# The first stage of a decoder block on one core: products nobody reads ahead of the tokens, earlier weight requests, a projection in three sweeps, forget sums first, values early

## The chip, the cores and the metric

The kernel runs on one core of a Trainium2 chip. The metric is the device time of one execution in microseconds (us). Engines: PE (TensorE), DVE (VectorE), ACT (ScalarE), POOL (GpSimd) and SP (SyncE, which here issues most DMA transfers).

## What is computed

The reference is one decoder block over 512 tokens of 1024 channels, in fp32, with one layer. The first half mixes tokens in three branches and adds the result to x; the second half is an expert retrieval.

```python
h = rmsnorm(x, norm1_g[l])
z = h @ w_in[l]
fq, fk, fv, ff, sq, sk, sv, mq, gl = jnp.split(z, splits, axis=-1)
fq = head_rmsnorm(fq.reshape(B, S, FOX_HEADS, FOX_HD), fox_q_g[l])
fk = head_rmsnorm(fk.reshape(B, S, FOX_HEADS, FOX_HD), fox_k_g[l])
log_f = jax.nn.log_sigmoid((ff + b_forget[l]).astype(jnp.float32))
o_fox = fox_attention(fq, fk, fv, log_f)      # causal, scores + cumsum(log_f)
o_swa = swa_attention(sq, sk, sv, swa_sinks[l], slopes)   # window 128, ALiBi
mn = rmsnorm(mem, mem_norm_g[l])
mk, mv = jnp.split(mn @ w_mem_kv[l], 2, axis=-1)
o_mem = memory_attention(mq, mk, mv)          # 256 memory rows
merged = gates[:, :, 0] * (o_fox @ w_fox_o[l]) + ...
x = x + merged @ w_out[l]
x = x + peer_ffn(rmsnorm(x, norm2_g[l]), ...) # top 16 of 128 x 128 experts, 8 heads
```

## The kernel before

The 512 tokens are four blocks of 128. The mixers run twice: for block 0 alone (group 0) and for blocks 1 to 3 (group 1). The expert search and the fetching of expert rows for block 0 are woven into group 1's mixers; then follow the search for blocks 1 to 3 and a long dense part over all experts for blocks 2 and 3. Up to the end of that search a scheduler with a model of the times sets the order of the instructions on each engine, from the dependences and the order in which the program states them; from the dense part on, PE, DVE and POOL follow the program's own order.

Products that need more than the PE's fast format are made from two parts each: `whi` is the weight rounded by a cast on ACT (`load`, L118), `wlo` the rest, by a subtraction on DVE or POOL (`rest`, L130), and `mm3` (L144 to L146) adds whi x own, wlo x own and whi x ownlo. The weights come as pairs of halves of 512 KB (`raw`, L112); `whi` and `wlo` have three buffers each.

The start of group 0, which the change touches: x of block 0 is fetched, its squares are summed on ACT (`squares`, L197), POOL makes the factor (L191), ACT a diagonal matrix of it (`dg`, L211), and PE turns x by eight products with `dg` (`turn`, L224). ACT and DVE evict each turned chunk into `own` (L225) and `ownlo` (L227). `skvf` then projects to the window keys and values and the eight forget logits (264 columns, w_skvf); its logits become a log-sigmoid (L401 to L404) and a running sum `cum` (L409, L410). `fox_qkv(0, 0)` makes keys, queries and values of the first four forgetting heads (w_nat; 256 columns each); keys and queries carry `cum` as two more columns (L447, L449) and are turned into `kT` and `qT` (L348, L349). `memory` turns the 256 memory rows in the same way as x (`dg` of two blocks, `mT`) and projects them. `fox` attends; `fox_qkv(0, 1)` does the other four heads.

Of the kernel before, what the change touches and what calls it, by code (L numbers as in the profile page):

```python
# [49 lines left out]
AHEAD, ROWS_IN, MORE = 4, 5, 2  # L50
LATER = 400
# [5 lines left out]
def tile_block(ctx: ExitStack, tc: tile.TileContext, t: dict, out: bass.AP):  # L57
# [41 lines left out]
    early, loads = [], [0]  # L99
# [14 lines left out]
    def load(src, n, w, fetch=None):  # L114
# [3 lines left out]
        A.copy(hi[:, :n * w], raw[:, :n * w])  # L118
        return raw[:, :n * w], hi[:, :n * w], n, src.shape[0] if len(src.shape) == 3 else 1
# [15 lines left out]
    def load_split(src, n, w, pool=None, fetch=None):  # L135
        return rest(load(src, n, w, fetch), share[0] if pool is None else pool)
# [37 lines left out]
    nc.sync.dma_start(cst[:, 0], t["c_mats"][:, 0])  # L174
# [62 lines left out]
    first_w = [load_raw(t["w_skvf"][half], 4 * 264) for half in range(2)]  # L237
    nc.sync.dma_start(cst[:, 1:], t["c_mats"][:, 1:])
    pre = ExitStack()
    pp = pre.enter_context(tc.tile_pool(name="pp", bufs=2))  # L240
# [23 lines left out]
    distb = pp.tile([128, 256], BF16, name="distb", bufs=1)  # L264
    slope = pp.tile([128, 8, 128], BF16, name="slope", bufs=1)
    raw = wp.tile([128, WSLOT], F32, tag="raw", name="raw")
    nc.sync.dma_start(raw[:, :256], t["c_dist"])
    V.tensor_copy(distb, raw[:, :256])
    for h in range(8):
        A.mul(slope[:, h], ident, 2.0 ** -(h + 1))  # L270

    def gemm_nat(lhs, src, n, nb, use, more=None, fetch=None):

        w = [load_split(src[half], 4, n, fetch=fetch) for half in range(2)]
# [37 lines left out]
    def heads(lhs, src, nb, nh, hd, pad=0, n=None, also=None, fetch=None):  # L312
# [12 lines left out]

        gemm_nat(lhs, src, n or nh * hd, nb, use, fetch=fetch)
# [58 lines left out]

    def skvf(g, hT):
# [9 lines left out]
        skn = heads(hT, t["w_skvf"], nb, 2, 64, n=264, also=also, fetch=(lambda src, n: first_w.pop(0)) if g == 0 else None)  # L396
# [4 lines left out]
        A.activation(ab, xf[:, bs], AF.Abs)  # L401
        A.activation(ab, ab, AF.Exp, scale=-1.0)
        A.activation(ab, ab, AF.Ln, bias=1.0)
        V.scalar_tensor_tensor(xf[:, bs], xf[:, bs], 0.0, ab, op0=OP.min, op1=OP.subtract)  # L404
        ps = bank("tg")
        for i, b in enumerate(bl):
            for j in range(b):
                PE.matmul(ps[:, i * 8:i * 8 + 8], ones, xf[:, j], start=j == 0, stop=False)
            PE.matmul(ps[:, i * 8:i * 8 + 8], tri, xf[:, b], start=b == 0, stop=True)  # L409
        V.tensor_copy(cum[:, bs].rearrange("p b h -> p (b h)"), ps[:, :nb * 8])  # L410
# [27 lines left out]
    def fox_qkv(g, c, hT):  # L438
# [3 lines left out]
        if g == 0:  # L442
            fkT[c] = pp.tile([128, 4, S], F32, tag="kT", name="kT")
            fv[c] = pp.tile([128, NB, 256], F32, tag="v", name="v")
        kn = heads(hT, t["w_nat"][3 * c], nb, 4, 64, pad=2)
        V.memset(kn[:, :, :, 64], 1.0)
        V.tensor_scalar(kn[:, :, :, 65], cum[:, bs, hs], -1.0, None, op0=OP.mult)  # L447
# [146 lines left out]
    def mixers(g, hT):  # L594
# [731 lines left out]
```

## Time and profile before

| | us |
|---|---|
| median of 3 runs | 1600.31 (1598.24 to 1602.07) |
| the profiled execution, its time | 1592.0 |
| its span in the trace | 1590.2 |
| PE busy | 1506.6 |
| DVE busy | 1427.9 |
| ACT busy | 833.7 |
| PE busy in the first 50 us | 34.1 |

The profile was taken in one execution; "busy" is the time in which an engine ran an instruction, and a row of the timeline gives start, length, engine, source line, operation, output and inputs, and in brackets the engine's idle time before it and what ended that. PE's single rows overlap, since products are pipelined: the pitch from start to start tells its pace. A four-byte product of 128 columns by the slow format appears as two records.

### The profile page before, as it was taken

To read this page: it belongs to the slowest core of one execution; us is meant where nothing else is said; L and a number is where in the kernel's file an instruction comes from. 1 tells how busy PE (TensorE), PEld (TensorE's weight loads), DVE (VectorE), ACT (ScalarE), POOL (GpSimd) and SP (SyncE) were. 2 spreads that over 40 slices of the span, in tenths; PEclk is the share of its full clock that TensorE was granted. 3 is DMA by queue.
4 is the path that set the end of the run, shared out by engine and by line. 5 is a ranking of instruction groups with operands and counts; after the bars stand their busy time and mean duration, and the time that the engine had idled before them with its cause. 6 is when DMAs were issued, how large, how long until landed. Compare 5 with 4: busy or idle time off the path is not lost.

```text
span 1590.2 us, 27117 instructions
## 1 busy us (share of the span) xinstructions
PE 1506.6 (95%) x9422; PEld 1370.9 (86%) x9422; DVE 1427.9 (90%) x2663; ACT 833.7 (52%) x1838; POOL 779.5 (49%) x639
## 2 busy tenths in 40 slices
PE   6999999999998989999995999899999999999998
PEld 5999899898897989999884999688888888888887
DVE  5677477989999989999899999799999999999998
ACT  7787426656445433454314998554454444454443
POOL 1100015777566456457844666445455454555451
PEclk9999999999998999999997999999999999999999
DMA  8586766899998799965797999999999999999995
GB/s 304 180 279 220 237 214 225 317 355 322 331 356 303 262 355 332 378 245 177 256 412 270 379 402 389 362 407 407 401 409 410 406 410 408 409 409 407 410 409 213
DMA packets 178361, 531.90 MB, mean 334 GB/s; under 512 B 17456, under 2 KB 46384, under 8 KB 178224
## 3 DMA queue, kind: packets, MB, share of 16 engines
q0 software_dynamic: 73728, 268.47, 44.6%
q1 hardware_dynamic: 94704, 226.04, 38.9%
q10 hardware_dynamic: 9792, 35.66, 5.6%
q8 instruction: 74, 1.21, 0.3%
q14 instruction: 63, 0.52, 0.1%
HBM read 515.42 MB, written 14.68 MB: 333 GB/s over the span
## 4 chain that ended last, share of the span: by engine, by line
PE 46%; DMA 17%; issue 15%; POOL 10%; DVE 9%; ACT 3%; SPq 0%; POOLq 0%; DVEq 0%; ACTq 0%
PE mm L999 9%; POOL row L838 9%; DMA row<-in_peer_u_dram,eidx 7%; DMA row<-in_peer_v_dram,eidx 7%; PE mm L145 6%; PE mm L146 6%; PE mm L144 6%; PE sc L1073 3%; DVE wlo L130 2%; DMA raw<-in_peer_v_dram 1%; PE mm L716 1%; PE sc L145 1%; PE sc L146 1%; PE tp L145 1%; PE sc L144 1%
## 5 line engine op out<-in xcount | busy, mean ns | idle before, releaser
L838 POOL DMA_INDIRECT row<-in_peer_v_dram,eidx x256 | 323.3, 1263 | 285.0 <-DVE two L866 163.9
L838 POOL DMA_INDIRECT row<-in_peer_u_dram,eidx x256 | 318.6, 1244 | 232.0 <-DVE scr L853 124.5
L130 DVE TENSOR_TENSOR wlo<-raw,whi 128x1024 fp32r<-128x1024 f32 (+1 forms) x244 | 300.7, 1234 | 33.4 <-ACT whi L118 29.5
L866 DVE SCALAR_TENSOR_TENSOR two<-row,acts,two 128x1024 f32<-128x1024 f32 x176 | 226.2, 1285 | 2.5 <-DMA row<-in_peer_v_dram,eidx 0.2
L118 ACT CAST whi<-raw 128x1024 fp32r<-128x1024 f32 (+1 forms) x148 | 154.9, 1049 | 106.5 <-PE mm L145 73.4
L853 DVE SCALAR_TENSOR_TENSOR scr<-row,own 128x1024 bf16<-128x1024 f32 x128 | 156.2, 1220 | 20.7 <-DMA row<-in_peer_u_dram,eidx 19.9
L853 DVE SCALAR_TENSOR_TENSOR scr<-row,two 128x1024 bf16<-128x1024 f32 x117 | 142.3, 1216 | 3.3 <-DMA row<-in_peer_u_dram,eidx 2.0
L191 POOL TENSOR_TENSOR rsy<-rsv,mhalf 128x4 f32<-128x4 f32 (+5 forms) x25 | 38.3, 1535 | 191.4 <-DVE rsv L190 172.1
L1126 ACT CAST ah<-ga 128x256 fp32r<-128x256 f32 x116 | 47.1, 407 | 155.9 <-PE tp L145 126.3
L1128 ACT CAST whi<-raw 128x1024 fp32r<-128x1024 f32 x96 | 100.4, 1047 | 21.0 <-DMA raw<-in_peer_v_dram 15.5
L144 PE MATMUL mm<-hhi,whi 128*128 128x384 f32 x320 | 110.0, 344 | 1.2 <-DVE mg L643 0.7
L145 PE MATMUL mm<-hlo,whi 128*128 128x384 f32 x320 | 109.8, 343 | 0.0
L146 PE MATMUL mm<-hhi,wlo 128*128 128x384 f32 x320 | 109.7, 343 | 0.0
L145 PE MATMUL sc<-wlo,ah 128*128 128x512 f32 x256 | 101.5, 396 | 5.8 <-DVE wlo L130 5.8
L144 PE MATMUL mm<-whi,hhi 128*128 128x256 f32 (+1 forms) x360 | 103.7, 290 | 1.5 <-DVE mg L643 1.0
L145 PE MATMUL mm<-wlo,hhi 128*128 128x256 f32 (+1 forms) x360 | 103.0, 287 | 1.2 <-DVE wlo L130 1.1
L146 PE MATMUL mm<-whi,hlo 128*128 128x256 f32 (+1 forms) x360 | 102.3, 286 | 0.6 <-DVE hlo L632 0.6
L146 PE MATMUL sc<-whi,al 128*128 128x512 f32 x256 | 101.2, 395 | 0.0
L144 PE MATMUL sc<-whi,ah 128*128 128x512 f32 x256 | 100.7, 393 | 0.0
L145 PE MATMUL tp<-wlo,ah 128*128 128x512 f32 x256 | 100.7, 393 | 0.0
L144 PE MATMUL tp<-whi,ah 128*128 128x512 f32 x256 | 100.6, 393 | 0.0
L146 PE MATMUL tp<-whi,al 128*128 128x512 f32 x256 | 100.2, 391 | 0.0
(301 smaller groups left out, 4535.7 us busy)
## 6 DMA issues: line engine op xcount, KB each, us to landing
raw<-in_peer_v_dram SPq DMA_DIRECT2D x96, 512.0 KB, 7.8
hhi<-in_uT_dram ACTq DMA_DIRECT2D x68, 512.0 KB, 7.6
raw<-in_w_tr_dram SPq DMA_DIRECT2D x48, 512.0 KB, 5.2
raw<-in_w_nat_dram SPq DMA_DIRECT2D x40, 512.0 KB, 5.4
last<-in_peer_v_dram SPq DMA_DIRECT2D x32, 512.0 KB, 7.1
hhi<-in_uT_dram SPq DMA_DIRECT2D x26, 512.0 KB, 7.1
raw<-in_w_o_dram SPq DMA_DIRECT2D x24, 512.0 KB, 5.6
gd<-st SPq DMA_DIRECT2D x24, 512.0 KB, 12.1
```

Of the source, the lines that this page charges most:

```text
L118: A.copy(hi[:, :n * w], raw[:, :n * w])
L130: V.tensor_sub(lo, raw, hi.bitcast(F32))
L144: PE.matmul(ps, lh, rh, start=first, stop=False)
L145: PE.matmul(ps, lh, rl, start=False, stop=False)
L146: PE.matmul(ps, ll, rh, start=False, stop=last)
L838: G.indirect_dma_start(out=r, out_offset=None, in_=t["peer_" + tab], in_offset=bass.IndirectOffsetOnAxis(ap=eidx[b][:, j:j + 1], axis=0))
L853: V.scalar_tensor_tensor(scr, r, 1.0, two[0] if b else h2n[b], op0=OP.mult, op1=OP.mult, accum_out=acts[b][:, c]))
L866: V.scalar_tensor_tensor(two[0], r, acts[b][:, c], two[0], op0=OP.mult, op1=OP.add))
L999: PE.matmul(ps[:, :TD], w[:, dc], h2f[dc], start=dc == 0, stop=dc == KC - 1)
L1073: PE.matmul(ps[:, u], o[:, 1, u], o[:, 0, u], start=True, stop=True)
L1126: A.copy(ah, a)
L1128: A.copy(hi, raw)
```

## The change

- Ahead of everything PE makes 36 products of 256 columns from a cleared bf16 tile (`distb`, cleared on DVE) into a bank that nothing reads.
- The identity matrix (`cst`) and the gains (`gcol`) are asked for on ACT's queue, and the two halves of w_skvf directly behind x on SP's.
- The first turning takes its eight chunks through banks of all tags instead of two.
- For group 0 the casts of w_skvf go to DVE, and its 24 products are made in three sweeps of eight (whi x own, wlo x own, whi x ownlo) in place of three per chunk.
- The slopes and distances of the window attention are made behind the memory stage (`biases`).
- The forget logits are evicted by ACT, then the bias is added on DVE; the steps to `cum` and its copies into keys and queries have high priority for group 0.
- For group 0 the values of all eight heads are projected in `fox_qkv(0, 0)`.

```diff
+    pre = ExitStack()
+    pp = pre.enter_context(tc.tile_pool(name="pp", bufs=2))
+    distb = pp.tile([128, 256], BF16, name="distb", bufs=1)
+    V.memset(distb, 0.0)
+    unread = bank("mm")
+    for _ in range(UNREAD):
+        PE.matmul(unread[:, :256], distb[:, :128], distb, start=True, stop=True)
...
-    nc.sync.dma_start(cst[:, 0], t["c_mats"][:, 0])
+    nc.scalar.dma_start(cst[:, 0], t["c_mats"][:, 0])
...
-    nc.sync.dma_start(gcol, t["g_cols"])
+    tc.keep_in_program_order(nc.scalar.dma_start(gcol, t["g_cols"]))
+    first_w = []
+    for half in range(2):
+        first_w.append(wp.tile([128, WSLOT], F32, tag="raw", name="raw"))
+        tc.keep_in_program_order(nc.sync.dma_start(first_w[-1], t["w_skvf"][half]))
...
-    first_w = [load_raw(t["w_skvf"][half], 4 * 264) for half in range(2)]
...
-    norm_t([xg[:, 0]], xsum, g1, *hT)
+    norm_t([xg[:, 0]], xsum, g1, *hT, tags=("tp", "sc", "tp", "sc", "tg", "acc", "mm", "tp"))
...
-    A.copy(hi[:, :n * w], raw[:, :n * w])
+    (cast or A.copy)(hi[:, :n * w], raw[:, :n * w])
...
+            if cast:
+                for i, (lt, rt) in enumerate(((0, 0), (0, 1), (1, 0))):
+                    for dc in range(KC):
+                        PE.matmul(ps, lhs[lt][dc][:, tok], w[dc // 4][rt][:, dc % 4],
+                                  start=i == dc == 0, stop=i == 2 and dc == KC - 1)
+                use(b, ps)
+                continue
...
-            V.tensor_add(xf[:, bl[b]], ps[:, 256:264], b_forget)
+            A.copy(xf[:, bl[b]], ps[:, 256:264])
+            with urgent(g):
+                V.tensor_add(xf[:, bl[b]], xf[:, bl[b]], b_forget)
...
-        gemm_nat(hT, t["w_nat"][3 * c + 2], 256, nb, lambda b, ps: A.copy(fv[c][:, bl[b]], ps))
+        for i in (c,) if g else ((0, 1) if c == 0 else ()):
+            if g == 0:
+                fv[i] = pp.tile([128, NB, 256], F32, tag="v", name="v")
+            gemm_nat(hT, t["w_nat"][3 * i + 2], 256, nb, lambda b, ps: A.copy(fv[i][:, bl[b]], ps))
...
         if g == 0:
             memory()
+            biases()
```

How the instructions stand. The lines of the changed program are some 10 to 30 higher. First PE, from the first turning of x (`tp`, `sc`, ... are banks; `dg` the diagonal matrix; `mg_78` x) on; before:

```order
L224 MATMUL tp<-dg,mg_78 128x128
L224 MATMUL sc<-dg,mg_78 128x128
L224 MATMUL tp<-dg,mg_78 128x128
L224 MATMUL sc<-dg,mg_78 128x128
L144 MATMUL mm<-whi,own 128x264
L145 MATMUL mm<-wlo,own 128x264
L224 MATMUL tp<-dg,mg_78 128x128
L146 MATMUL mm<-whi,ownlo 128x264
L144 MATMUL mm<-whi,own 128x264
L145 MATMUL mm<-wlo,own 128x264
L144 MATMUL mm<-whi,own 128x256
```

The same place of PE in the changed program, behind the 36 unread products:

```order
L236 MATMUL sc<-dg,mg_78 128x128
L236 MATMUL tg<-dg,mg_78 128x128
L236 MATMUL acc<-dg,mg_78 128x128
L236 MATMUL mm<-dg,mg_78 128x128
L292 MATMUL mm<-whi,own 128x264 x3
L236 MATMUL tp<-dg,mg_78 128x128
L292 MATMUL mm<-whi,own 128x264 x5
L292 MATMUL mm<-wlo,own 128x264 x8
L292 MATMUL mm<-whi,ownlo 128x264 x7
L145 MATMUL mm<-whi,own 128x256
L292 MATMUL mm<-whi,ownlo 128x264
```

Seven of the eight turnings stand ahead of the first product of the projection, the eighth behind three products; the next projection (256 columns) begins one product ahead of the end of the third sweep.

Then ACT, between the two diagonal steps, of x and of the memory. Before, the last rows up to the memory's (`ab` are the log-sigmoid's steps, `whi` the weight casts):

```order
L401 ACTIVATE ab<-xf 128x8
L118 CAST whi<-raw 128x1024
L402 ACTIVATE ab<-ab 128x8
L118 CAST whi<-raw 128x1024
L349 ACTIVATE skT<-tg,gcol 128x128
L319 COPY qn<-mm 128x4x64
L321 ACTIVATE sq<-mm 128x256
L403 ACT_TABLE_LOAD
L403 ACTIVATE ab<-ab 128x8
L118 CAST whi<-raw 128x1024
L451 COPY v<-mm 128x256
L118 CAST whi<-raw 128x1024
```

After them come the two `dg` and `kT`. In the changed program, the last rows ahead of `dg` and the rows behind it:

```order
L119 CAST whi<-raw 128x1024 x3
L367 ACTIVATE skT<-tg,gcol 128x128
L337 COPY qn<-mm 128x4x64
L339 ACTIVATE sq<-mm 128x256
L209 ACTIVATE junk,sums<-mg_471 128x1024 x2
L480 COPY v<-mm 128x256
L119 CAST whi<-raw 128x1024
L367 ACTIVATE kT<-tg,gcol 66x4x128
L223 ACTIVATE dg<-cst,rsy 128x128 x2
L119 CAST whi<-raw 128x1024
L367 ACTIVATE qT<-tg,gcol 66x4x128
L119 CAST whi<-raw 128x1024
```

`kT` stands ahead of `dg` now, the memory's squares (`junk`) directly before, and casts follow behind it where before the turned memory's evictions did. From `dg` of x to `dg` of the memory there were 11 casts on ACT (two of them of w_skvf) and there are 8.

Last SP, from x of block 0 on, before:

```order
L173 DMA mg_78<-in_x_dram 128x512 x2
L174 DMA cst<-in_c_mats_dram 128x128
L177 DMA gcol<-in_g_cols_dram 128x46
L112 DMA raw<-in_w_skvf_dram 128x1056 x2
L238 DMA cst<-in_c_mats_dram 128x512
L248 DMA hb<-in_b_gate_cols_dram 128x24
L256 DMA grow<-in_g_rows_dram 128x16
L267 DMA raw<-in_c_dist_dram 128x256
L112 DMA raw<-in_w_nat_dram 128x1024 x5
L416 DMA mg_404<-in_mem_dram 128x1024 x2
L112 DMA raw<-in_w_nat_dram 128x1024
```

and now:

```order
L174 DMA mg_78<-in_x_dram 128x512 x2
L189 DMA raw<-in_w_skvf_dram 128x1056 x2
L249 DMA cst<-in_c_mats_dram 128x512
L257 DMA hb<-in_b_gate_cols_dram 128x24
L265 DMA grow<-in_g_rows_dram 128x16
L113 DMA raw<-in_w_nat_dram 128x1024 x7
L441 DMA mg_471<-in_mem_dram 128x1024 x2
L113 DMA raw<-in_w_nat_dram 128x1024
L113 DMA raw<-in_w_mem_dram 128x1024 x8
```

The two small loads are gone from between x and w_skvf, the distances from ahead of w_nat, and seven halves of w_nat, not five, stand ahead of the memory's rows.

More of the change, by code (lines that the diff above doesn't have):

```diff
@@ L50 @@
 AHEAD, ROWS_IN, MORE = 4, 5, 2
+UNREAD = 36
 LATER = 400
@@ L97, in tile_block @@
     due, share = [0.0], [0.0]
-    early, loads = [], [0]
+    early, loads = [], [2]
     def load_raw(src, n):
@@ L112, in fill, with load @@
             nc.sync.dma_start(raw[:, :n], src)
-    def load(src, n, w, fetch=None):
+    def load(src, n, w, fetch=None, cast=None):
         pump()
@@ L133, in rest, with load_split @@
         return [x.rearrange("p (n w) -> p n w", n=n) for x in (hi, lo)]
-    def load_split(src, n, w, pool=None, fetch=None):
-        return rest(load(src, n, w, fetch), share[0] if pool is None else pool)
+    def load_split(src, n, w, pool=None, fetch=None, cast=None):
+        return rest(load(src, n, w, fetch, cast), share[0] if pool is None else pool)
     def split(hi, lo, src):
@@ L261, in tile_block, with biases, gemm_nat @@
     V.tensor_scalar(nsink, sinks, -1.0, None, op0=OP.mult)
-    distb = pp.tile([128, 256], BF16, name="distb", bufs=1)
     slope = pp.tile([128, 8, 128], BF16, name="slope", bufs=1)
[L266 to L274, printed above, removed]
+    def biases():
+        raw = pp.tile([128, 256], F32, tag="sq", name="dist")
+        nc.sync.dma_start(raw, t["c_dist"])
+        V.tensor_copy(distb, raw)
+        for h in range(8):
+            tc.keep_in_program_order(A.mul(slope[:, h], ident, 2.0 ** -(h + 1)))
+    def gemm_nat(lhs, src, n, nb, use, more=None, fetch=None, cast=None):
+        w = [load_split(src[half], 4, n, fetch=fetch, cast=cast) for half in range(2)]
         for b in range(nb):
@@ L310, in gemm_tr, with heads @@
         return ps
-    def heads(lhs, src, nb, nh, hd, pad=0, n=None, also=None, fetch=None):
+    def heads(lhs, src, nb, nh, hd, pad=0, n=None, also=None, fetch=None, cast=None):
         z = pp.tile([128, BIG, 4 * 66], F32, tag="qn", name="qn")
@@ L324, in use @@
                 also(b, ps)
-        gemm_nat(lhs, src, n or nh * hd, nb, use, fetch=fetch)
+        gemm_nat(lhs, src, n or nh * hd, nb, use, fetch=fetch, cast=cast)
         r = rsqrt_mean(ss, nb * nh, hd)
@@ L384, in tile_block, with urgent @@
     cum = consts.tile([128, NB, 8], F32, name="cum")
+    def urgent(g):
+        return tc.high_priority(LATER) if g == 0 else ExitStack()
     def skvf(g, hT):
@@ L393, in also @@
             A.copy(sv[:, bl[b]], ps[:, 128:256])
-            V.tensor_add(xf[:, bl[b]], ps[:, 256:264], b_forget)
-        skn = heads(hT, t["w_skvf"], nb, 2, 64, n=264, also=also, fetch=(lambda src, n: first_w.pop(0)) if g == 0 else None)
+            A.copy(xf[:, bl[b]], ps[:, 256:264])
+            with urgent(g):
+                V.tensor_add(xf[:, bl[b]], xf[:, bl[b]], b_forget)
+        first = dict(fetch=lambda src, n: first_w.pop(0), cast=V.tensor_copy) if g == 0 else {}
+        skn = heads(hT, t["w_skvf"], nb, 2, 64, n=264, also=also, **first)
         tr_heads(skT[:, :, bl[0] * 128:(bl[0] + nb) * 128], skn, g_sk,
@@ L400, in skvf @@
         ab = small.tile([128, BIG, 8], F32, tag="ab", name="ab", bufs=2)[:, :nb]
[L401 to L410, printed above, removed]
+        with urgent(g):
+            A.activation(ab, xf[:, bs], AF.Abs)
+            A.activation(ab, ab, AF.Exp, scale=-1.0)
+            A.activation(ab, ab, AF.Ln, bias=1.0)
+            V.scalar_tensor_tensor(xf[:, bs], xf[:, bs], 0.0, ab, op0=OP.min, op1=OP.subtract)
+            ps = bank("tg")
+            for i, b in enumerate(bl):
+                for j in range(b):
+                    PE.matmul(ps[:, i * 8:i * 8 + 8], ones, xf[:, j], start=j == 0, stop=False)
+                PE.matmul(ps[:, i * 8:i * 8 + 8], tri, xf[:, b], start=b == 0, stop=True)
+            V.tensor_copy(cum[:, bs].rearrange("p b h -> p (b h)"), ps[:, :nb * 8])
     def memory():
@@ L443, in fox_qkv @@
             fkT[c] = pp.tile([128, 4, S], F32, tag="kT", name="kT")
-            fv[c] = pp.tile([128, NB, 256], F32, tag="v", name="v")
         kn = heads(hT, t["w_nat"][3 * c], nb, 4, 64, pad=2)
         V.memset(kn[:, :, :, 64], 1.0)
-        V.tensor_scalar(kn[:, :, :, 65], cum[:, bs, hs], -1.0, None, op0=OP.mult)
+        with urgent(g):
+            V.tensor_scalar(kn[:, :, :, 65], cum[:, bs, hs], -1.0, None, op0=OP.mult)
         qn = heads(hT, t["w_nat"][3 * c + 1], nb, 4, 64, pad=2)
-        V.tensor_copy(qn[:, :, :, 64], cum[:, bs, hs])
+        with urgent(g):
+            V.tensor_copy(qn[:, :, :, 64], cum[:, bs, hs])
         V.memset(qn[:, :, :, 65], 1.0)
-        gemm_nat(hT, t["w_nat"][3 * c + 2], 256, nb, lambda b, ps: A.copy(fv[c][:, bl[b]], ps))
+        for i in (c,) if g else ((0, 1) if c == 0 else ()):
+            if g == 0:
+                fv[i] = pp.tile([128, NB, 256], F32, tag="v", name="v")
+            gemm_nat(hT, t["w_nat"][3 * i + 2], 256, nb, lambda b, ps: A.copy(fv[i][:, bl[b]], ps))
         tr_heads(fkT[c][:, :, bl[0] * 128:(bl[0] + nb) * 128], kn, g_fk,
```

2 lines of the change are left out of this document (removed).

## The prediction

> **What bounds the kernel now.** I read the page first: the span, the share of each engine, and the chain that ended last.
>
> ```profile
> span 1590.2 us, 27117 instructions
> PE 1506.6 (95%) x9422; PEld 1370.9 (86%) x9422; DVE 1427.9 (90%) x2663; ACT 833.7 (52%) x1838; POOL 779.5 (49%) x639
> PE 46%; DMA 17%; issue 15%; POOL 10%; DVE 9%; ACT 3%; SPq 0%; POOLq 0%; DVEq 0%; ACTq 0%
> ```
>
> PE is busy 95% of the span, so a change gains only where PE waits or runs slowly. The second view is the busy time by stretch (length, then PE, PEld, DVE, ACT, POOL, granted clock, DMA share, GB/s).
>
> ```profile
> 0.00:7.50 7.50, 0.00 (x0) 0.00 (x0) 0.65 (x5) 4.98 (x17) 0.76 (x5) 1.00 0.65 230
> 7.50:18.20 10.70, 8.84 (x37) 8.24 (x38) 6.79 (x15) 6.67 (x14) 0.00 (x0) 1.00 1.01 374
> 18.20:30.00 11.80, 10.13 (x80) 9.43 (x78) 8.88 (x18) 11.22 (x22) 2.76 (x2) 1.00 0.97 381
> 30.00:34.00 4.00, 0.98 (x4) 0.54 (x4) 2.95 (x8) 1.49 (x3) 2.31 (x2) 0.73 0.86 277
> 34.00:38.70 4.70, 3.88 (x18) 3.45 (x18) 1.12 (x3) 2.85 (x6) 0.42 (x1) 0.50 0.47 165
> 38.70:50.00 11.30, 10.27 (x87) 9.72 (x87) 5.37 (x13) 7.60 (x20) 0.00 (x0) 1.00 0.07 14
> 50.00:100.00 50.00, 49.95 (x413) 48.88 (x413) 34.06 (x53) 40.46 (x78) 5.65 (x5) 1.00 0.75 260
> 100.00:140.00 40.00, 37.53 (x278) 33.87 (x277) 31.84 (x60) 31.49 (x72) 4.55 (x5) 0.97 0.80 260
> 140.00:180.00 40.00, 39.53 (x307) 38.36 (x307) 27.96 (x42) 25.18 (x43) 0.00 (x0) 0.99 0.70 228
> 500.00:620.00 120.00, 109.63 (x647) 106.21 (x648) 110.50 (x151) 47.25 (x91) 68.52 (x51) 0.92 0.87 305
> ```
>
> From 50 to 180 us PE is full (49.95 of 50, then 37.53 of 40 and 39.53 of 40). The loss lies ahead of that: nothing at all until 7.5 us, a stall at 30 to 34, and half the clock in the two stretches after 30 us. Since the later stages wait on engines and buffers and on no point in time, I take what the first 50 us save to reach the end. The third view is the time order of the first 50 us.
>
> ```profile
> 5.49 0.58 POOL L191 TENSOR_TENSOR rsy<-rsv,mhalf 128x1 f32<-128x1 f32 x1 [5.05 <-DVE rsv L190]
> 6.14 1.09 ACT L270 ACTIVATE slope<-cst 128x128 bf16<-128x128 f32 x5
> 7.14 0.39 ACT L211 ACTIVATE dg<-cst,rsy 128x128 f32<-128x128 f32 x1
> 7.58 0.79 PE L224 MATMUL tp<-dg,mg 128*128 128x128 f32 x2 [7.58 <-ACT dg L211]
> 7.85 1.07 ACT L118 CAST whi<-raw 128x1056 fp32r<-128x1056 f32 x1 [0.33 <-DMA raw<-in_w_skvf_dram]
> 10.12 0.36 ACT L225 ACTIVATE own<-tp,gcol 128x128 fp32r<-128x128 f32 x1
> 11.84 0.35 DVE L227 SCALAR_TENSOR_TENSOR ownlo<-tp,gcol,own 128x128 fp32r<-128x128 f32 x1
> 12.10 0.34 DVE L227 SCALAR_TENSOR_TENSOR ownlo<-sc,gcol,own 128x128 fp32r<-128x128 f32 x1
> 17.64 0.41 PE L145 MATMUL mm<-wlo,own 128*128 128x256 f32 x1
> 17.85 0.42 PE L146 MATMUL mm<-whi,ownlo 128*128 128x256 f32 x1
> 18.49 0.28 PE L144 MATMUL mm<-whi,own 128*128 128x264 f32 x1
> 18.61 0.28 PE L145 MATMUL mm<-wlo,own 128*128 128x264 f32 x1
> 19.94 0.28 PE L146 MATMUL mm<-whi,ownlo 128*128 128x264 f32 x1
> 24.89 1.07 ACT L118 CAST whi<-raw 128x1024 fp32r<-128x1024 f32 x1
> 25.94 1.07 ACT L118 CAST whi<-raw 128x1024 fp32r<-128x1024 f32 x1
> 31.59 0.16 DVE L410 COPY cum<-tg 128x8 f32<-128x8 f32 x1
> 33.02 1.06 PE L348 MATMUL tg<-cst,qn 128*66 128x128 f32 x4 [3.04 <-DVE qn L447]
> 34.45 0.69 ACT L211 ACTIVATE dg<-cst,rsy 128x128 f32<-128x128 f32 x2 [2.96 <-POOL rsy L191]
> 34.91 2.07 PE L224 MATMUL tp<-dg,mg 128*128 128x128 f32 x8 [0.82 <-ACT dg L211]
> 35.05 0.67 ACT L349 ACTIVATE kT<-tg,gcol 66x512 f32<-66x512 f32 x1
> ```
>
> PE's products follow each other every 0.21 us at 17.64 and every 0.12 us at 18.49: until about 18.2 us it ran at half speed, although the granted clock is printed as 1.00 there. It does so again up to 38.7 us, after the stall. That stall is 3.04 us for the running sums of the forget logits, whose copy (L410) stands at 31.59. The memory's turning begins at 34.45, when its two diagonal matrices (dg) can be made.
>
> **The unread products, and PE's start.** 36 products of 256 columns now stand ahead of PE's first real work. At the slow pitch (17.64 to 17.85) all of them take 36 x 0.21 = 7.6 us, and if half run at the fast pitch 36 x 0.165 = 5.9 us. They need only a memset, so they begin at about 0.9 us and end between 6.8 and 8.5. The real work was ready late: POOL's factor ended at 6.07, but the first dg waited behind five slopes on ACT (6.14) until 7.14. The slopes are moved away, so dg can end at about 6.5, and PE is held by the unread products to perhaps 7.4. The first own on ACT stood at 10.12, behind two weight casts of 1.07 us each that go to DVE now; it comes about 0.5 us after PE begins, at 7.9. Bounds: 7.0 with no hold, 9.0 with the whole slow batch ahead of it.
>
> [...]
>
> **Moved requests.** Two small loads leave SP's queue for ACT's, so the first weights are asked for two places earlier; at SP's pitch below that is 0.9 us.
>
> ```profile
> 1.64 0.42 SPq L174 DMA_DIRECT2D cst<-in_c_mats_dram  x1
> 2.58 0.91 SPq L112 DMA_DIRECT2D raw<-in_w_skvf_dram  x2
> 10.13 0.22 DVE L259 CAST causb<-cst 128x128 bf16<-128x128 f32 x1
> 10.46 0.29 DVE L268 CAST distb<-raw 128x256 bf16<-128x256 f32 x1
> 10.67 1.25 DVE L130 TENSOR_TENSOR wlo<-raw,whi 128x1056 fp32r<-128x1056 f32 x1
> ```
>
> The bytes stay the same and the DMA share is 1.01 from 7.5 to 18.2, so this gains little by itself: the first cast waited only 0.33 us for them. ACT issues its two ahead of its table load and has nothing else to do before x lands, so they cost nothing; without that cover, about 0.9 us. The distances (a load behind SP's weights) leave the head of the queue, which brings the next weights earlier.
>
> **Three sweeps.** The 24 products are the same, but the eighth turning now stands behind three of them on PE and waits for DVE's first ownlo, which stands behind two casts and one wlo there. No row has DVE casting 1056 columns. From 128 to 256 columns a cast rises from 0.22 to 0.29, which extends to 0.75 us, an estimate; above, it is bounded by the two-operand wlo, 1.25 us. I take 0.75, the same kind of operation. The first weights landed at 7.85, so now at 6.9: 6.9 + 0.75 + 1.25 + 0.75 = 9.65, where the first ownlo can begin. Eight of them at 0.25 (the pitch of the rows at 11.84 and 12.10), the second wlo at 1.25 and 0.3 for two small steps make 13.2, so the third sweep ends near 13.5 us. Before, this projection's last product stood at 19.94, mixed with the next one's. The price is that the first weights are held until the third sweep: there are three whi buffers, so the second cast of the next projection waits for it, about 1.3 us on ACT.
>
> **What sets the middle: ACT.** Between the two dg steps ACT was busy 6.67 + 11.22 + 1.49 = 19.4 us of the 26.5 from 7.5 to 34. In the changed order 8 casts stand there where 11 stood (the pitch is 25.94 - 24.89 = 1.05, so -3.2), one more small copy (+0.2) and the kT eviction (+0.65, somewhat under the 0.67 of its row): 17.1 us. From 7.9 that gives 25.0 without any wait. ACT's waits were 7.1 us before; I take 3, the 1.3 above, 0.4 for the third sweep's end, and the rest for PE's pace. So dg stands at 28.0 instead of 34.45, **6.4 us** earlier. Bounds: 9.4 with no wait, 2.3 with all 7.1. The forget sums are ready before that; what is late next is the memory's squares on ACT, not they.
>
> **The second slow stretch.** PE's 3.88 busy us from 34 to 38.7 ran at half speed. If the clock stays up, half of it, 1.9 us, is saved where PE leads, nothing where ACT and DVE do; I take **1.3**, bounds 0 and 1.9.
>
> **Values early.** The second half's value projection, 24 products of 0.12 us, moves from the full stretch behind 50 us to where PE waits: at most 2.8 us. Its last 11 stand behind the memory's first turnings, so I take **2.5**, bounds 1.4 and 2.8. With the slopes, which come back behind the memory stage (1.09 us for five, so 1.7 for eight), and two casts fewer there, ACT is even later on (40.46 busy of 50).
>
> **The cost.** Four casts and the value copy now stand on ACT between dg and the memory's last eviction, where no cast stood: 4 x 1.05 + 0.3 = 4.5 us. ACT was idle 1.85 + 3.70 us there (34 to 50), so most is hidden: **-1.2**, bounds 0 and -4.5.
>
> The sum is 6.4 + 1.3 + 2.5 - 1.2 = 9.0 us. The profiled execution took 1592.0 us (its span is 1590.2), so that one would be 1583.0. The median shown, 1600.31, is 8.3 above it; I carry the saving over: **1591.3 us**. The terms' bounds do not fall together; combined as independent errors, with some 2 us for the spread of a median (runs from 1598.24 to 1602.07), the likeliest case lies between 1586 and 1597.
>
> **Rivals.** First, the clock falls back. After the unread products PE has only turnings and three sweeps until 13.5, far below half busy; the stall at 30 to 34 (0.98 busy of 4) did drop it, while 10.13 of 11.8 kept it. A clock that falls there wastes the warming. The sweeps and the first two halves of weights would run slowly: 24 + 24 products with 0.09 us more each is 4.3 us, and a repeated slow stretch in the memory stage takes back the 1.3; ACT and DVE hide about 1.5. That leaves 9.0 - 4.1 = 4.9, so 1595.4 us. [...]
>
> Second, the gain does not reach the end. The instructions of the mixers for the other three blocks and of the search come in another order on PE, DVE and ACT too, from about 370 us to behind 660, though no operation of theirs changes. If the row fetches set the pace there (DMA 17% and POOL 10% of the chain), an earlier start only makes PE wait longer: 1600 us. Against it: PE is busy 109.63 of 120 in that stretch.
>
> Third, slower: the clock in that reordered stretch. It was 0.92 granted over 500 to 620, so 16% of the 120 us, 19 us, ran at half speed, with PE 91% busy. [...] To outweigh 9.0 it takes more than 18 us of added half clock, as much again as now; with 25 us the loss is 12.5, so 1603.8 us. Nothing in the rows points to so much.
>
> **How the numbers follow.** The forecast has 0.56, the clock rival 0.20, the absorbed gain 0.14, the slower order 0.10. A measurement of this kernel tells 0.2%, 3.2 us, from no change: faster means under 1597.1. The forecast falls there nearly always (0.53 of 0.56), the clock rival in nine of ten (0.18), the absorbed gain seldom (0.02): 0.73 faster. Slower takes most of the third rival and a little of the second: 0.10. The rest, 0.17, is no change. For the range I reach down to 1585.5 and up to 1600.5, which takes in the clock rival and the absorbed gain and leaves the slow order out.
>
> **What would show it.** Right: PE's products at 0.12 us apart from its first real turning on; the first projection done by about 13.5 us; the memory's dg near 28 us; no granted clock of 0.50 between 30 and 39; and PE full from about 40 us. Wrong: own later than 9 us (the unread products in the way); a clock of 0.50 between 8 and 25 us; ACT idle for over 6 us before dg; or a first stage that ends 9 us earlier while the span does not, which would put the loss into the reordered stretch behind 370 us.

## The result, and the profile after

| | before | changed |
|---|---|---|
| median | 1600.95 us (12 runs) | 1589.28 us (12 runs) |
| ratio, 95% interval | | 0.9937 (0.9921 to 0.9952) |
| saved | | 10.1 us (7.7 to 12.6) |
| span of the profiled execution | 1590.2 us | 1592.1 us |

The change is faster by its interval, and 1591.3 us was forecast. The saving is worked out from the ratio; the two medians differ by 11.7 us. One run on each side that was disturbed (2486 and 8472 us) is left out of the ratio. The two profiled spans cannot be set against each other: a second profile of the kernel before has a span of 1603.1 us, 13 us more than the first, and the changed kernel's own first profile, at 1593.83 us, has the longest of the eleven times in its ratio. So the comparison goes by points in the program that both traces share, and by the ratio. The experiments ran on three chips, on which the kernel before has medians of 1601.83, 1599.18 and 1596.22 us, so each time below has its ratio to before on the same chip.

The page of the changed kernel (span; busy time of the engines):

```profile
span 1592.1 us, 27209 instructions
PE 1514.5 (95%) x9458; PEld 1374.6 (86%) x9458; DVE 1433.5 (90%) x2666; ACT 829.5 (52%) x1840; POOL 779.0 (49%) x639
```

Nothing of the change shows there; it shows by stretch. The changed kernel, in the columns of the prediction's table (length; PE, PEld, DVE, ACT, POOL busy; granted clock; DMA share; GB/s):

```profile
7.50:18.20 10.70, 8.58 (x66) 7.77 (x65) 10.49 (x22) 7.77 (x20) 0.46 (x1) 1.00 1.04 411
...
30.00:34.00 4.00, 2.90 (x26) 2.69 (x26) 3.70 (x7) 3.98 (x7) 0.00 (x0) 1.00 0.79 281
34.00:38.70 4.70, 4.16 (x37) 3.93 (x36) 2.61 (x8) 3.69 (x15) 0.00 (x0) 1.00 0.72 218
38.70:50.00 11.30, 11.25 (x97) 11.01 (x96) 6.07 (x13) 8.83 (x19) 1.01 (x1) 1.00 0.65 232
50.00:100.00 50.00, 46.88 (x377) 45.06 (x376) 34.98 (x58) 39.96 (x87) 7.68 (x5) 0.97 0.70 235
100.00:140.00 40.00, 39.59 (x288) 36.73 (x289) 31.84 (x55) 29.74 (x64) 2.21 (x3) 0.95 0.72 227
```

PE executes 66 products between 7.5 and 18.2 us where it had executed 37, it is busy 2.90 us of the old stall (0.98), and 30 to 38.7 us run at full clock. But from 50 to 100 us, where PE was full (49.95), 3.1 us are lost now.

The time order of the changed kernel's first 30 us:

```profile
1.04 6.14 PE L182 MATMUL mm<-distb 128*128 128x256 bf16 x36 [1.04 <-DVE mhalf L196]
1.64 0.90 SPq L189 DMA_DIRECT2D raw<-in_w_skvf_dram  x2
6.49 0.40 ACT L223 ACTIVATE dg<-cst,rsy 128x128 f32<-128x128 f32 x1 [0.80 <-POOL rsy L203]
7.47 0.37 ACT L237 ACTIVATE own<-tp,gcol 128x128 fp32r<-128x128 f32 x1 [0.58 <-PE tp L236]
7.66 0.71 DVE L119 CAST whi<-raw 128x1056 fp32r<-128x1056 f32 x1 [1.87 <-DMA raw<-in_w_skvf_dram]
10.20 0.34 DVE L239 SCALAR_TENSOR_TENSOR ownlo<-tp,gcol,own 128x128 fp32r<-128x128 f32 x1
10.60 0.49 PE L236 MATMUL tp<-dg,mg 128*128 128x128 f32 x2 [1.46 <-DVE ownlo L239]
13.77 1.05 ACT L119 CAST whi<-raw 128x1024 fp32r<-128x1024 f32 x1 [1.33 <-PE mm L292]
14.05 0.28 PE L292 MATMUL mm<-whi,ownlo 128*128 128x264 f32 x1
24.92 0.15 DVE L435 COPY cum<-tg 128x8 f32<-128x8 f32 x1
27.73 0.68 ACT L223 ACTIVATE dg<-cst,rsy 128x128 f32<-128x128 f32 x2
```

The first projection ends at 14.3 us, the running sums are copied at 24.92 instead of 31.59, and the memory's dg starts at 27.73 instead of 34.45.

The point that carries the comparison is the first product of the output projection of the first group's mixers, a place where all of that group's earlier products are done. Before:

```profile
174.97 1.99 PE L297 MATMUL mm<-raw,own 128*128 128x256 f32 x8 [0.47 <-ACT own L628]
```

Changed:

```profile
167.41 3.72 PE L315 MATMUL mm<-raw,own 128*128 128x256 f32 x16 [0.47 <-ACT own L658]
```

7.6 us earlier. The experiments below speak of this point as "the projection". Where part of the saving was given back shows in the changed kernel's waits from 60 to 105 us (in total, times, longest) and in the granted clock behind them. The wait for `wlo`, the low part of a weight, falls at 66 and 75 us; the one for `qn`, here the normalised queries of the window, at 96.5 us:

```profile
PE mm L146 <- DVE wlo L131: 1.5, 2, 0.8
PE tg L366 <- DVE qn L348: 1.2, 1, 1.2
```

```profile
93.98:97.39 3.41, 1.80 (x16) 1.40 (x15) 2.40 (x7) 2.03 (x8) 1.88 (x1) 1.00 0.87 306
95.00:100.00 5.00, 3.77 (x23) 3.08 (x22) 2.30 (x9) 3.62 (x10) 0.86 (x1) 0.74 0.63 225
100.00:105.00 5.00, 5.00 (x25) 4.47 (x26) 3.25 (x6) 1.33 (x3) 0.00 (x0) 0.57 0.39 115
```

A granted clock of 0.74 over 5 us and 0.57 over the next 5 is 2 x (0.26 + 0.43) x 5 = 6.9 us at half speed (the stretch from 97.39 to 104.21 us by itself has 0.50), which costs a full PE 3.4 us.

### The profile page after: what moved, and what is told of

Read it like the earlier page. It is cut to its first block, busy times and chain, and to the rows that moved or that the text cites. A ratio compares the mean times of both kernels' runs of the same rounds, so it can differ in the third digit from the quotient of the medians.

```text
span 1592.1 us, 27209 instructions
## 1 busy us (share of the span) xinstructions
PE 1514.5 (95%) x9458; PEld 1374.6 (86%) x9458; DVE 1433.5 (90%) x2666; ACT 829.5 (52%) x1840; POOL 779.0 (49%) x639
## 4 chain that ended last, share of the span: by engine, by line
PE 54%; DVE 13%; issue 12%; DMA 11%; POOL 6%; ACT 4%; DVEq 0%; POOLq 0%; SPq 0%; ACTq 0%
PE mm L146 8%; PE mm L1029 8%; PE mm L147 8%; PE mm L145 8%; DMA row<-in_peer_v_dram,eidx 5%; POOL row L868 4%; DMA row<-in_peer_u_dram,eidx 4%; DVE wlo L131 3%; PE sc L1103 3%; DVE two L896 2%; PE sc L146 1%; PE sc L147 1%; PE sc L145 1%; PE tp L145 1%; PE tp L146 1%
## 5 line engine op out<-in xcount | busy, mean ns | idle before, releaser
L131 DVE TENSOR_TENSOR wlo<-raw,whi 128x1024 fp32r<-128x1024 f32 (+1 forms) x244 | 304.2, 1248 | 33.6 <-ACT whi L119 26.5
L119 ACT CAST whi<-raw 128x1024 fp32r<-128x1024 f32 x146 | 152.6, 1050 | 100.4 <-PE mm L146 62.4
L1158 ACT CAST whi<-raw 128x1024 fp32r<-128x1024 f32 x96 | 100.4, 1048 | 18.2 <-DMA raw<-in_peer_v_dram 12.7
```

The lines of the kernel that those rows point to most:

```text
L119: (cast or A.copy)(hi[:, :n * w], raw[:, :n * w])
L131: V.tensor_sub(lo, raw, hi.bitcast(F32))
L1158: A.copy(hi, raw)
```

## The experiments

**The two kernels unaltered, profiled again.**

> The kernel before, unchanged, profiled a second time. Theory A (the gain is made ahead of 50 us and carried to the end): the first stage repeats, the memory's diagonal step (dg) within 1 us of 34.45 and the first product of w_out for block 0 within 2 us of 175.0; what differs between two profiles of one kernel lies behind 200 us and is some 5 us. Theory C (the middle is as fixed as the first stage): the span repeats within 2 us of 1590.2.

> The changed kernel, unchanged, profiled a second time. Theory A: dg of the memory within 1 us of 27.73, the first product of w_out within 2 us of 167.4, and the span anywhere from 1584 to 1593. Theory C: the span within 2 us of 1592.1.

Measured: the memory's dg at 34.58 us before and 27.62 changed, the projection at 174.6 and 165.8 (a third profile of the change, below, has 167.2). The first stage repeats as theory A has it; its 5 us for what differs later was too small, since the spans of before differ by 13. The dense part's first step (L1058) stands at 856.7 and 862.1 before, and at 852.2, 849.5 and 850.3 changed. So the mean saving is 8.0 us at the projection and 8.7 us at the start of the dense part, 680 us later, and 10.1 at the end by the ratio: by these means it is made in the first stage, and carried. The two profiles of before lie 5.4 us apart at the dense part, so a microsecond or two there means nothing.

**Without the unread products.**

```diff
-UNREAD = 36
+UNREAD = 0
```

> The changed kernel without the 36 unread products; nothing else is edited. Theory A (ACT paces the first 28 us): PE's first projection runs at the slow pitch, but ACT hides most of it; dg of the memory comes 0.5 to 2 us later than 27.73, and the time grows by 1 to 3 us over the changed kernel (0.995 to 0.996 of the time before). Theory B (the clock is the main part of the gain): dg at 31 or later, the clock drops again behind it, and the time grows by 5 us or more (0.997 or above).

Measured: 1595.49 us, ratio 0.9955 (0.9938 to 0.9973); the projection at 167.4. The last product of the third sweep starts at 18.80 us instead of 14.05, and the memory's dg came 5.4 us later than in the change:

```profile
14.02 1.81 PE L292 MATMUL mm<-wlo,own 128*128 128x264 f32 x8
18.80 0.28 PE L292 MATMUL mm<-whi,ownlo 128*128 128x264 f32 x1
33.10 0.70 ACT L223 ACTIVATE dg<-cst,rsy 128x128 f32<-128x128 f32 x2
```

Turnings and sweeps at half clock are what the warming avoids; the second sweep takes 1.81 us instead of 1.47, with a granted clock of 0.50 from 14.20 to 17.61. But dg at 33.10, nearly as late as before, went with a projection 7.4 us earlier than before. Theory B had this dg, theory A this time: the end does not follow dg. The interval of the ratio overlaps the change's.

**The unread products alone, on the kernel before.** The diff is the change's first block, with nothing else.

> The kernel before with the 36 unread products alone. Theory A: the products of the first projection come at the fast pitch, but the stall for the forget sums and ACT's 11 casts stay; dg of the memory at 32 to 34 and a gain of 0.5 to 2.5 us (0.9985 to 0.9997). Theory B: dg at 30 or earlier and 5 us or more of gain (0.997 or below).

Measured: 1601.03 us, ratio 0.999 (0.9978 to 1.0001), the projection at 175.7. Warming alone gains nothing that can be measured. In the trace the clock falls back (stretches 8 to 14 and 14 to 20 us), and the memory's dg at 36.06 us is later than both theories had it:

```profile
8.00:14.00 6.00, 2.25 (x13) 1.84 (x12) 4.47 (x10) 3.92 (x9) 0.00 (x0) 0.82 0.97 355
14.00:20.00 6.00, 6.00 (x34) 6.00 (x34) 3.38 (x7) 2.20 (x5) 0.00 (x0) 0.61 1.03 417
```

2 x (0.18 + 0.39) x 6 = 6.8 us at half clock (0.50 from 11.79 to 18.62): what the first rival expected, in a kernel where the weights are still cast on ACT and PE has only 2.25 us of work between 8 and 14 us.

**The values where they were, in the changed kernel.**

```diff
-        for i in (c,) if g else ((0, 1) if c == 0 else ()):
+        for i in (c,):
```

> The changed kernel, with the second half's values projected where they were before. Theory A (the gain is what PE neither waits nor runs at half speed before the first stage's output projection; it is carried from there): the 24 products of 0.12 us no longer fill PE's waits between 30 and 39 us, where PE was busy 7.07 of 8.70, so PE should show about 4.3 to 5 busy us there and the first product of the output projection should stand at 169 to 169.5 us (175.0 and 174.6 before, 167.4 and 165.8 in the two profiles of the change). Ratio to before 0.995 to 0.9965. Theory B (the memory's dg step sets what follows): dg stays at 27.5 to 28, the projection at 166 to 167.5, ratio 0.993 to 0.994. Theory C (the values only move PE's wait: the 3.1 us that PE lost between 65 and 100 us come from there): PE is full again from 65 to 100 us (34.5 of 35 or more), the projection at 166 to 167.5.

Measured: 1593.24 us, ratio 0.9959 (0.9944 to 0.9974), the projection at 170.9. A row of PE in this kernel, and the same row before:

```profile
131.89 0.44 PE L366 MATMUL tg<-cst,qn 128*128 128x128 f32 x2 [1.54 <-DVE qn L348]
135.94 0.44 PE L348 MATMUL tg<-cst,qn 128*128 128x128 f32 x2 [1.56 <-DVE qn L330]
```

The change's wait of 1.2 us for the window's queries at 96.5 us is gone: here 20 products of the first branch's output stand between the window's first scores and that turning, and in the change none. In its place PE waits 1.5 us for the memory's queries at 132 us, as before, where the change does not wait. So the early values bring the instructions into another order and move a wait, they do not add one: all nine profiles with early values have 1.2 to 1.8 us near 100 us, and all five without have 1.5 or 1.6 near 134. The wait for `wlo` stays, and PE is busy 32.84 of 35 us from 65 to 100, not full as theory C had it; the ratio is theory A's. This profile also has half clock early (0.50 from 11.07 to 14.49 and from 34.97 to 38.38 us) where the change's three have none, so its 170.9 overstates the worth of the values.

**The early values alone, on the kernel before.** The same line the other way, with the buffers for both halves.

> The kernel before, with nothing of the change but the early values of the second half. Theory A: they fill waits between 30 and 50 us, where PE was idle 4.9 us of 20, so the output projection begins 2 to 2.5 us earlier, at 172.3 to 172.8 instead of 174.8, ratio 0.998 to 0.999. Theory C: PE waits between 65 and 100 us for what it saved, the projection begins at 174.5 to 175, ratio 1.000. Against both: the four more casts between dg and the last eviction cost ACT up to 4.5 us, the projection at 176 or later.

Measured: 1592.33 us, ratio 0.9957 (0.994 to 0.9973), the projection at 170.4. This one edit, costed at 2.5 us, brings 4.4 by the projection and 6.9 (4.3 to 9.6) by the time; the unread products, the other part that was run alone, bring nothing. Taken out of the change, in the run above, the early values cost 3.0 to 3.5 us by the ratios, with intervals that overlap; so their worth may depend on what else is there. Its old stall, and the memory's dg:

```profile
30.00:34.00 4.00, 3.28 (x29) 3.19 (x27) 2.98 (x8) 3.49 (x6) 1.25 (x1) 1.00 0.94 320
34.00:38.70 4.70, 2.95 (x23) 2.27 (x22) 3.67 (x7) 3.99 (x8) 1.64 (x2) 1.00 0.79 278
35.67 0.69 ACT L211 ACTIVATE dg<-cst,rsy 128x128 f32<-128x128 f32 x2
```

PE is busy 3.28 us of the four instead of 0.98, and the clock does not fall behind them. The memory's dg is 1.2 us later than before (35.67), and the end is earlier all the same.

**Without sweeps and casts on DVE.**

```diff
-        first = dict(fetch=lambda src, n: first_w.pop(0), cast=V.tensor_copy) if g == 0 else {}
+        first = dict(fetch=lambda src, n: first_w.pop(0)) if g == 0 else {}
```

> The changed kernel, with the first weights cast on ACT again and their products in the order of before (one chunk after another, three products each). Theory A with the clock: behind the unread products PE has only turnings until the first chunks, own stands near 9.9 us, so the clock falls back at 11 to 12 us for 6.8 us as it did with the unread products alone (half of 6.8 is 3.4 us at most, some of it hidden); with two casts of 1.07 us more on ACT the memory's dg comes at 30 to 32 us and the output projection at 169 to 171, ratio 0.996 to 0.998. Theory D (the sweeps gain nothing, since 24 products are 24 products): dg at 28, projection at 166 to 167.5, ratio 0.993 to 0.994, no granted clock below 1.00 between 8 and 25 us.

Measured: 1588.56 us, ratio 0.9937 (0.9918 to 0.9955), the projection at 167.5.

```profile
8.91 1.07 ACT L119 CAST whi<-raw 128x1056 fp32r<-128x1056 f32 x1
9.89 0.36 ACT L237 ACTIVATE own<-tp,gcol 128x128 fp32r<-128x128 f32 x1
18.92 0.28 PE L147 MATMUL mm<-whi,ownlo 128*128 128x264 f32 x1
```

own stands behind both casts again, the granted clock is 0.50 from 13.17 to 16.59 us, and the first projection ends 4.9 us later. By the trace sweeps and casts together are worth some 3.5 us (the table below); by the time they are worth nothing that six runs can tell. Theory D has this time; the half clock and the memory's dg (32.16) are nearer to theory A. The place of sweeps and casts in the gain stays open.

**The head of the program as before** (the small loads on SP, slopes and distances ahead of the first turnings).

```diff
-    nc.scalar.dma_start(cst[:, 0], t["c_mats"][:, 0])
+    nc.sync.dma_start(cst[:, 0], t["c_mats"][:, 0])
-    tc.keep_in_program_order(nc.scalar.dma_start(gcol, t["g_cols"]))
+    tc.keep_in_program_order(nc.sync.dma_start(gcol, t["g_cols"]))
+    biases()        # where slope is made
-            biases()
```

> The changed kernel, with the head of the program as before: the two small loads asked for by SP ahead of the first weights, and distances and slopes made where they were, ahead of the first turnings. Theory A with the sum of the prediction: the weights land about 0.9 us later, dg of the first turnings 0.6 us later behind the slopes; the first projection ends about 0.9 us later (15.2 instead of 14.3), the output projection at 167.3 to 168.3, ratio 0.994 to 0.995. Rival E (the bytes are the same and the DMA engines are full, so the order of the requests gives nothing): the first cast at 7.6 to 7.8 as in the change, the projection at 166 to 167.5, ratio 0.993 to 0.994. Against both: the distances' load behind the weights, the second weights later by over 2 us and a stall on PE near 20 us: projection at 170 or later.

Measured: 1588.43 us, ratio 0.9942 (0.9926 to 0.9957), the projection at 163.4, the earliest of all.

```profile
2.58 0.91 SPq L189 DMA_DIRECT2D raw<-in_w_skvf_dram  x2
7.63 0.71 DVE L119 CAST whi<-raw 128x1056 fp32r<-128x1056 f32 x1 [2.26 <-DMA raw<-in_w_skvf_dram]
11.26 0.17 DVE L270 TENSOR_SCALAR nsink<-grow 128x8 f32<-128x8 f32 x1 [0.61 <-DMA grow<-in_g_rows_dram]
```

The weights are asked for 0.94 us later than in the change (2.58 against 1.64) and land at the same time (7.63 against 7.66): rival E was right on that. What is asked for behind them does land later: DVE waits 0.61 us for the small load `grow` between two ownlo, and the first projection ends at 15.2 us, as theory A had it. The run on the slopes alone, below, differs from this one in the requests only; there it ends at 14.5, and the memory's dg stands at 27.89 instead of 28.58. So the order of the requests is worth 0.7 us there, too little for the times to tell.

That the projection is 4.0 us earlier than the change's is mostly luck with the clock: no half clock falls ahead of it in this profile, 6.9 us (3.4 us lost) in the change's. The 0.6 us left is what the slopes bring less what the requests cost.

**Unread products and early values, nothing else.** Both diffs above on the kernel before.

> The kernel before, with two parts of the change only: the unread products and the early values. Theory F (these two make the gain; sweeps, DVE casts, moved requests and the priority of the forget sums add under 1 us): the output projection of the first stage begins at 167 to 168.5 us (167.5 in the change without its sweeps), ratio to before 0.993 to 0.9955. Theory G (the sweeps are what makes the warm clock of use; with early values alone the ratio was 0.9957, and unread products alone gave 0.999): the clock falls back at about 12 us for 6.8 us, the projection begins at 169.5 to 171, ratio 0.9955 to 0.9975.

Measured: 1590.42 us, ratio 0.9962 (0.9948 to 0.9975), the projection at 170.5; the change itself, on the same chip, 1587.01. The clock fell back early, for 2 x (0.19 + 0.10) x 6 = 3.5 us (0.50 from 11.75 to 15.17):

```profile
8.00:14.00 6.00, 2.66 (x14) 2.25 (x13) 5.17 (x11) 4.19 (x9) 0.00 (x0) 0.81 0.98 349
14.00:20.00 6.00, 6.00 (x48) 5.99 (x46) 3.09 (x8) 3.58 (x6) 0.00 (x0) 0.90 1.04 418
```

Theory G, which expected 6.8 us of half clock, fits better than F, in the projection, the clock and the ratio; the intervals overlap with the change's.

**24 unread products in the stall,** at the place of the early values, on the kernel before.

```diff
+        if g == 0 and c == 0:
+            full = bank("mm")
+            for _ in range(24):
+                PE.matmul(full[:, :256], distb[:, :128], distb, start=True, stop=True)
```

> The kernel before, with 24 unread products of 256 columns added at the place where the change has the second half's values, and nothing else; it leaves out nothing. They cost PE 24 x 0.11 = 2.6 us in the stall at 30 to 34 us, where it waited about 3 us, and bring no work forward. Theory H (a good part of what the early values bring is that the clock does not fall: 6.8 us at half speed from 32 us on): granted clock 1.00 from 30 to 39 us, output projection at 172.5 to 173.5 us instead of 174.8, ratio 0.998 to 1.000. Theory I (it is the moved work alone): projection at 174.5 to 176, ratio 0.9995 to 1.0015, whatever the clock does.

Measured: 1596.21 us, ratio 0.9996 (0.9981 to 1.0011), the projection at 172.0. PE's rows, then the stretch 34 to 38.7 us:

```profile
29.26 2.58 PE L455 MATMUL mm<-distb 128*128 128x256 bf16 x22
34.68 0.63 PE L348 MATMUL tg<-cst,qn 128*66 128x128 f32 x4 [2.49 <-DVE qn L447]
34.00:38.70 4.70, 4.02 (x22) 3.63 (x23) 1.57 (x6) 3.09 (x7) 0.55 (x1) 0.67 0.49 187
```

The filler was done at 31.8 us, with 2.49 us of stall still to come, and the clock fell behind it. The run therefore does not separate the kept clock from the moved work; it shows only that filler which ends ahead of the stall's end gains no time that can be told. Its projection is 2.8 us earlier than before's, 1.7 of it because the half clock near 138 us (0.50 from 137.65 to 141.06 before) is missing in this profile; the time does not follow, so a single projection foretells the end only roughly.

**The slopes early, the requests as in the change.** Of the diff for the head, only the last two lines.

> The changed kernel, with the distances and the eight slopes made where they were, ahead of the first turnings, and the requests as in the change. Theory J (in the change the eight slopes, 1.71 us on ACT at 62 us, hold a weight cast back, for which PE then waits 1.5 us between 65 and 75 us): that wait is gone, PE is busy 33.3 of 35 us or more from 65 to 100, the output projection begins at 163 to 165 us if no half clock falls ahead of it, and the time is about 1.5 us under that of the change, ratio 0.992 to 0.9935, too little for these medians to tell. Rival: the wait comes back elsewhere, since ACT is late by its casts and not by the slopes: PE 31.5 to 32.2 of 35, projection at 164 to 167.5, ratio as the change's.

Measured: 1587.56 us, ratio 0.995 (0.9933 to 0.9966), the projection at 164.1. First the change, on ACT, DVE and PE, then this kernel's waits and its stretch from 65 to 100 us:

```profile
62.01 1.71 ACT L281 ACTIVATE slope<-cst 128x128 bf16<-128x128 f32 x8
63.62 1.04 ACT L119 CAST whi<-raw 128x1024 fp32r<-128x1024 f32 x1
64.69 1.23 DVE L131 TENSOR_TENSOR wlo<-raw,whi 128x1024 fp32r<-128x1024 f32 x1 [2.05 <-ACT whi L119]
65.97 0.39 PE L146 MATMUL mm<-wlo,own 128*128 128x256 f32 x1 [0.85 <-DVE wlo L131]
```

```profile
PE tg L368 <- DVE qn L350: 1.2, 1, 1.2
65.00:100.00 35.00, 33.38 (x260) 31.54 (x259) 27.09 (x47) 29.37 (x64) 6.09 (x4) 0.95 0.80 266
```

Slopes, cast, `wlo`, product: the first of the two waits for `wlo` is a chain that the moved slopes begin, and both, 1.5 us, are gone when the slopes are made early (1.6 us lost from 65 to 100 instead of 3.1). In the median this is too little to be told from the change.

**The change once more, beside these.**

> The change itself, unaltered, on the chip of the last three and beside the same runs of before. Output projection at 164 us and half of what clock at half speed falls ahead of it, so 164 to 167.5; PE waits 1.5 us for the low part of a weight (L131) between 65 and 75 us; ratio 0.993 to 0.9945. By theory F it and the kernel with two parts alone lie within 2 us of each other, by theory G the change is 4 us or more ahead.

Measured: 1587.01 us, ratio 0.994 (0.9921 to 0.996), the projection at 167.2, with 6.8 us of half clock at 97 us again.

All kernels together; "without later half clock" takes off half of the half-clock time that lies between 60 us and the projection, where PE is otherwise full:

| kernel | memory's dg, us | projection, us | without later half clock | ratio of times |
|---|---|---|---|---|
| before, two profiles | 34.45, 34.58 | 175.0, 174.6 | 173.3, 172.9 | 1 |
| unread products alone | 36.06 | 175.7 | 174.0 | 0.999 |
| filler in the stall | 34.58 | 172.0 | 172.0 | 0.9996 |
| early values alone | 35.67 | 170.4 | 168.7 | 0.9957 |
| unread and early values | 34.21 | 170.5 | 167.1 | 0.9962 |
| change without early values | 28.58 | 170.9 | 169.2 | 0.9959 |
| change without sweeps | 32.16 | 167.5 | 167.5 | 0.9937 |
| change without unread | 33.10 | 167.4 | 167.4 | 0.9955 |
| change, three profiles | 27.73, 27.62, 27.57 | 167.4, 165.8, 167.2 | 164.0, 164.1, 163.8 | 0.9937, 0.994 |
| change, head as before | 28.58 | 163.4 | 163.4 | 0.9942 |
| change, slopes early | 27.89 | 164.1 | 162.4 | 0.995 |

The fourth column repeats within 0.4 us where a kernel was profiled more than once; the other kernels have one profile each, so it is no more than a guide for them. dg and the projection do not go together in it. No kernel is faster than the change by its interval.

## Why the prediction was right, point by point

**What bounds, and what is carried.** Right in the main: PE carries the saving to the end, 8.0 us at the projection and 10.1 at the end. It is not full from 40 us on, as was expected: it is up to 65 us (11.25 of 11.30 to 50), and loses 3.1 us between 65 and 100. The prediction also counted 37.53 of 40 as full. The second rival (absorbed from 370 us on) falls by the dense part's start, 8.7 us earlier in the mean, and 4.5 between the two nearest profiles. The third (more half clock in 500 to 620 us) falls by the granted clock there: 0.97, 0.96 and 0.97 in the three profiles of the change, 0.92 and 0.91 before.

**Unread products.** Right in its times. 36 products took 6.14 us and ended at 7.18; own followed at 7.47 (forecast 7.9). Their pace (stretches with PE's count of products):

```profile
1.04:3.04 2.00, 2.00 (x10) 1.44 (x11) 0.01 (x1) 1.28 (x1) 0.00 (x0) 1.00 0.56 175
5.30:7.10 1.80, 1.80 (x18) 1.61 (x17) 0.31 (x2) 0.79 (x6) 0.58 (x1) 1.00 0.94 350
```

From start to start they are 0.21 us apart at first and 0.11 from 5.3 us on, so 20 were slow; the prediction's 5.9 us took half of the 36 as slow.

**Moved requests.** The weights were to land 0.9 us earlier, at 6.9; they land at 7.66, 0.2 us earlier than before (7.85) and no earlier than when asked for 0.94 us later. The late weights made the first ownlo 0.55 us later than forecast (10.20 against 9.65) and the first projection's end 14.3 instead of 13.5. What the requests do bring, 0.7 us by the run with the old head, comes through a small load that the prediction had not counted.

**Three sweeps.** The details hold: 0.71 us for DVE's cast (0.75 estimated), 1.33 us for ACT's wait for a buffer (1.3). Their worth shows in the projection (167.5 against 164.0 without later half clock) and not in the median.

**ACT sets the middle, 6.4 us.** The forecast of the point was right, dg at 27.73 against 28.0, and taking it as the measure of the gain was wrong. With the early values alone dg is 1.2 us later than before and the projection 4.4 us earlier; without the unread products dg is 5.4 us later than in the change and the projection, by the fourth column, 3.4. PE does other work while it waits for dg. What the end follows is PE's own account: its idle time ahead of the projection (summed from the stretches up to it) was 18.9 us before and 10.3 in the change's first profile, and 6.1 of the 8.6 less were spent on the unread products. That leaves 2.5 of the 7.6 us between these two profiles; the other 5 are products no longer run at half clock. Counted directly, PE was busy at half clock for 17.1 us before (8.84 until 18.2 us, 4.83 from 31.85 to 38.67, 3.41 at 138) and for 6.8 in the change, beside the unread products: half of the difference is 5.1. So the sum of 9.0 came out right while its largest term named the wrong thing, and that it came so near to 10.1 is in good part luck. The forget sums were ready ahead of dg, as forecast (24.92); what the high priority has in that was not run, nor were the banks of all tags on their own.

**Second slow stretch 1.3, values 2.5.** The two belong together: the values fill the stall, and the clock stays behind it. Together they were put at 3.8; the early values alone on the kernel before bring 4.4. By the count above 1.2 us of it is less idle time and 3.0 less half clock against the first profile of before, 2.4 and 1.3 against the second; so how it divides is not settled, and the filler did not settle it.

**Cost.** The size was right by luck and the place wrong. ACT's casts behind dg cost nothing that shows: PE is busy 11.25 of 11.30 there. One edit was costed at nothing and cost PE a wait: the slopes behind the memory stage, 1.5 us ("ACT is even later on" was a mean over 50 us and hid a full stretch). The rest of the 3.1 us lost from 50 to 100 us, 1.6 for the window's queries, stands against 2.1 more busy us of PE from 100 to 140 (39.59 against 37.53), where the wait of 1.6 us for the memory's queries is gone. So 1.0 net, and the half clock at 97 us in place of that at 138.

**The first rival** (clock falling between 8 and 25 us) did not come true in the change. It did in all three kernels with unread products and without sweeps (6.8, 3.4 and 3.5 us at half clock), and in one of the six profiles with both, that of the late values. How near the change is to it, by two rows:

```profile
8.68:12.09 3.41, 1.95 (x14) 1.56 (x14) 3.41 (x8) 2.21 (x7) 0.00 (x0) 1.00 1.04 419
```

In the change PE was busy 1.95 us of that stretch and the clock stayed at 1.00 behind it; with the late values, in one that began 1.02 us earlier:

```profile
7.66:11.08 3.42, 1.83 (x14) 1.45 (x13) 3.07 (x7) 1.62 (x8) 0.00 (x0) 1.00 1.01 402
```

1.83 us, and the granted clock was 0.50 from 11.08 to 14.49. Only 0.12 us of PE's work lies between the two; more unread products between the turnings and the sweeps were not tried.

## What to carry to other kernels

Where PE stalls early, bring forward work from a later stage rather than filler, and then look in the trace at how the later order changed and where a wait went. Count PE's idle and half-clock time up to a point behind the whole stage, instead of the earlier start of one step ahead of it. Compare such points over several profiles: the projection repeats within two microseconds here, while whole spans of one kernel differ by 13.

## What the runs showed of the hardware

**The clock fell behind stretches in which PE was about half busy, not only behind nearly idle ones.** In the change PE was busy 1.80 of the 3.41 us from 93.98 to 97.39, with no wait over 1.23, and the granted clock was 0.50 from there to 104.21. With the late values 1.83 busy us from 7.66 to 11.08, and 2.01 from 31.56 to 34.97, had 0.50 behind them for 3.41 us each; without the sweeps it was 1.54 from 9.76 to 13.17, and with the unread products and early values alone 0.51 from 8.34 to 11.75. The busy time is the profile's, in which the ends of products are modelled.

It did not follow the same waits every time. Two kernels have the change's two (0.4 and 1.2 us): without the unread products, and with the head as before. In 3.41 us around them, from 96.12 and 93.61 us on, PE was busy 1.91 and 2.11 us, and the clock stayed at 1.00; why it did there was not shown. The second of them:

```profile
93.61:97.03 3.42, 2.11 (x18) 1.95 (x19) 1.92 (x8) 2.04 (x11) 1.20 (x1) 1.00 0.97 327
```

**On busy DMA engines an earlier request did not bring the first weights earlier:** 0.94 us apart in the asking, the two first casts started within 0.03 us of each other, with the DMA share at 0.92 from 2.58 to 7.63 us in the change. Behind them the order did count: the small load `grow`, asked for at 4.52 us with the head as before and at 3.88 in the change, held DVE up for 0.61 us there and not in the change.
